# The forgetting queries and keys as four pairs of seven quarter-block products behind the last mLSTM head

## The chip, the cores and the metric

The kernel runs on one core of a Trainium2 chip. The metric is the time of one execution on the device in microseconds (us), the median of several runs. The core has engines with instruction streams of their own: TensorE (PE, matmuls; PEld, its weight loads), VectorE (DVE), ScalarE (ACT), GpSimd (POOL), and SyncE (SP), which issues nearly all DMA transfers here. On chip there are SBUF, where operands live, and PSUM, eight banks of 128 x 512 float32 that matmuls write.

## The reference

One decoder layer on 1024 tokens of width 1024. The normed input is projected by `w_in`; four mLSTM heads and eight heads of forgetting attention share it. Then come an output projection, cross-attention to 256 memory tokens, an MLP with squared ReLU, and norms. The part that matters:

```python
h = rmsnorm(x, ln1[l])
z = h @ w_in[l]
ml_qk, ml_v, ml_o, ml_i, ml_f, fx_q, fx_k, fx_v, fx_f = jnp.split(z, splits, axis=-1)
...
fq = fx_q.reshape(B, S, FX_HEADS, FX_DH)
fk = fx_k.reshape(B, S, FX_HEADS, FX_DH)
fv = fx_v.reshape(B, S, FX_HEADS, FX_DH)
fx_out = forgetting_attention(fq, fk, fv, flf).reshape(B, S, FX_W)
```

`fx_q` and `fx_k` are 512 columns each: with the features in the partitions, four blocks of 128 x 1024 tokens for the queries and four for the keys. One such block holds two heads of 64.

## The kernel before

**Numbers in two parts.** A float32 operand is cut into a rounded part `hi` and the rest `lo` (`split`: ScalarE rounds, VectorE subtracts), and a product is three matmuls, lo x hi, hi x lo and hi x hi (`mm3`, lines 186 to 188). One matmul multiplies a 128 x 128 block of weights with up to 512 columns (tokens). `h` is the input times the gain `ln1`, cut, in two halves of 512 tokens; the norm's factor is put on afterwards, from `row` (tokens in the free dimension) or `rcol` (tokens in the partitions).

**Order.** The program is one straight list of Python calls. A planner puts each engine's instructions in an order, with the program's order as their rank, and an instruction that isn't ready lets later ones pass. Tiles come from groups with a name and a number of buffers: `act` 7 (128 x 8 x 512), `w4` 5 (128 x 1024), `z4` 2, weights `wr` 2 (raw), `wh` and `wl` 3 (cut), and tiles of 128 x 512 with the numbers of

```python
BUFS = dict(a=1, b=2, c=2, d=2, e=2, f=2, p=2, y=1)
PBUFS = dict(sc=3, mm=1, m2=1, tp=2, ov=1)
```

where the second line is the eight PSUM banks. In traces the tiles of the first line are `r_a`, `r_b` and so on, and `m2` is `m`.

**The heads' stage.** `ml_project(hd)` (line 656) projects one mLSTM head: keys with convolution (`conv_silu`), forgetting queries (`fx_project(0, hd)`, line 637), the state carried from the first half of the tokens (`carried`), queries with convolution, forgetting keys (`fx_project(1, hd)`), `carry`, and the output gate. `ml_head(hd)` (line 568) is the head itself: for each of its two halves of tokens it loads a row of maxima into a tile `a` (line 575), and for four to eight key blocks it makes scores in `sc` (584), exponentials (586), a mask on GpSimd (588), the weighted scores (589), cuts them, sums them on GpSimd (593) and multiplies by the values (595); at the end the sums over partitions (606, 607) and a factor. Then it yields; the rest, its closing, is drawn by `next(closing)`: the factors become a row through DRAM (`to_row`, 623, and the load at 625) in tiles `a`, and the output goes to `mix`. The loop calls the head, then `ml_project` of the next, in which the closing's three steps stand between the projections. The eight `fx_project` calls are spread over the four heads. Each multiplies one weight block with both halves of `h` (2 x 8 x 3 matmuls of 512 columns), scales by `row`, cuts, and stores both parts to `fqk` in DRAM.

**Behind the heads.** `fx_load` fetches queries, keys and decays of a forgetting head into a `stack` (an `act` tile, after memsets at 696 and 697). `slot` (line 1026) is one step of the forgetting attention; the first 13 (`LEAD_`) make scores only. `token_major(a["w_fv"], ...)` (488, called at 1092) makes the forgetting values, 2 x 8 blocks of 24 matmuls of 256 columns; `fv_sink` evicts them in turn into `b`, `p`, `c` (137, 138) and stores them (652). Head 3's closing is drawn in two of the slots and amid the values. The slots with values (782, 801) follow.

**Seven products elsewhere.** The cross-attention's queries and the first MLP product already use quarter blocks: `left_query` and `left_up` cut the weights, `right_side` prepares the right sides, and `Pair.run` adds the seven products up.

Of the kernel before, what the change touches and what calls it, by code (L numbers as in the profile page):

```python
# [9 lines left out]
F32 = mybir.dt.float32  # L10
F32R = mybir.dt.float32r
AF = mybir.ActivationFunctionType
ALU = mybir.AluOpType
# [4 lines left out]
P = 128  # L18
T = 1024
TH = 512  # L20
D = 1024
KT = D // P
# [3 lines left out]
FXD = 64  # L26
# [18 lines left out]
def hybrid_layer(ctx: ExitStack, tc: tile.TileContext, a: dict, out: bass.AP):  # L45
    nc = tc.nc
    v, s, g = nc.vector, nc.scalar, nc.gpsimd
# [39 lines left out]
    def ps_tile(tag):  # L87
        return psum.tile([P, 512], F32, tag=tag, name=name(tag), bufs=PBUFS[tag])
# [22 lines left out]
    load = nc.sync.dma_start  # L111
# [19 lines left out]
    def split(hi, lo, src, scale=None):  # L131

        if scale is None:
            s.activation(hi, src, AF.Copy)  # L134
            return v.tensor_tensor(out=lo, in0=src, in1=hi.bitcast(F32), op=ALU.subtract)  # L135
        else:
            s.activation(hi, src, AF.Copy, scale=scale)
            return v.scalar_tensor_tensor(out=lo, in0=src, scalar=scale, in1=hi.bitcast(F32), op0=ALU.mult, op1=ALU.subtract)  # L138

    spare = {}  # L140
    last_of = {}
# [42 lines left out]
    def mm3(ps, w, x, first, last, more=False):  # L184

        nc.tensor.matmul(ps, w[1], x[0], start=first, stop=False, skip_group_check=more)  # L186
        nc.tensor.matmul(ps, w[0], x[1], start=False, stop=False, skip_group_check=more)  # L187
        nc.tensor.matmul(ps, w[0], x[0], start=False, stop=last, skip_group_check=more)  # L188

    def both(pair, f):  # L190
        return f(pair[0]), f(pair[1])
# [233 lines left out]
    def row_first():  # L425
        to_row(row, rcol, 8, rowd[0:1])
# [25 lines left out]
    def gate_rows():  # L452
        ips = []
        for hf in range(2):
            ps = mm()
            for j in range(4):
                nc.tensor.transpose(ps[:GW, j * P : (j + 1) * P], lf[:, 4 * hf + j], ident)
            s.activation(steps[:, hf * TH : hf * TH + TH], ps[:GW], AF.Copy)
        for hf in range(2):
            ips.append(mm())  # L460
            for j in range(4):
                nc.tensor.transpose(ips[hf][:MLH, j * P : (j + 1) * P], z[:, 4 * hf + j, 0:MLH], ident)
        v.tensor_tensor_scan(out=cum, data0=on, data1=steps, initial=0.0, op0=ALU.mult, op1=ALU.add)
        for hf in range(2):
            c = slice(hf * TH, hf * TH + TH)
            v.tensor_tensor(out=rel[0:MLH, c], in0=ips[hf][:MLH], in1=cum[0:MLH, c], op=ALU.subtract)
        v.tensor_tensor_scan(out=run[0:MLH], data0=rel[0:MLH], data1=rel[0:MLH], initial=0.0, op0=ALU.max, op1=ALU.max)
        top = steps
        v.tensor_tensor(out=top[0:MLH], in0=cum[0:MLH], in1=run[0:MLH], op=ALU.add)
        neg = on  # L470
        v.tensor_scalar(out=neg[0:MLH], in0=run[0:MLH], scalar1=-1.0, scalar2=None, op0=ALU.mult)
        load(rows, neg[0:MLH])
        load(rels, rel[0:MLH, :TH])
# [11 lines left out]
                load(decay[sign, p_], cut[p_].bitcast(F32))  # L485


    def token_major(w_src, sink, cs=(0, 1), between={}):

        for c in cs:  # L490
            ws = [both(weights(w_src[c, i]), lambda t: t.rearrange("p (k c) -> p k c", k=4)) for i in range(2)]
            for t in range(8):
                if t in between:
                    between[t]()
                hf, tt = divmod(t, 4)
                ps = mm()[:, 0:256]
                for k in range(KT):
                    x = both(h[hf], lambda z: z[:, k, tt * P : (tt + 1) * P])
                    mm3(ps, x, both(ws[k // 4], lambda z: z[:, k % 4]), k == 0, k == KT - 1)
                sink(t, c, ps)  # L500

    def conv_silu(n, hi, lo):
        w = weights(a["w_in"][n])
# [130 lines left out]

    fqk = dram.tile([2, 2, 4, P, T], F32, name="fqk")

    def fx_project(which, n):
        w = weights(a["w_in"][12 + 4 * which + n])
        for _, hf, ps in proj(w, h, 1):
            lo = w2("p")  # L640
            v.scalar_tensor_tensor(out=lo, in0=ps, scalar=1.0 if which else FXD ** -0.5, in1=row[:, hf * TH : hf * TH + TH], op0=ALU.mult, op1=ALU.mult)
            hi = w2("p", dt=F32R)
            split(hi, lo.bitcast(F32R), lo)
            load(fqk[which, 0, n, :, hf * TH : hf * TH + TH], hi.bitcast(F32))
            load(fqk[which, 1, n, :, hf * TH : hf * TH + TH], lo)

    fvd = dram.tile([FXH, P, 8, 2 * FXD], F32, name="fvd")

    def fv_sink(t, c, ps):
# [28 lines left out]
    token_major(a["w_mv"], mv_sink, (1,), {2: row_first, 4: gate_rows})  # L678
    gate_cols()
    banks[:] = ["mm", "tp", "m2", "tp"]  # L680
    with tc.issue_after(last_sum.ins):
# [2 lines left out]
    for hd in range(MLH):  # L684
        closing = ml_head(hd, *ready)
        next(closing)
        if hd < MLH - 1:
            ready = ml_project(hd + 1)
    row_m = row[:, :NM]
    to_row(row_m, rcol_m, 2, rowd[1:2, :NM])  # L690

# [79 lines left out]
    class Values:  # L771
# [562 lines left out]
    def bank():  # L1334
        turn[0] += 1
        return ps_tile(cycle[turn[0] % 8])

    def sub(out_, x, y, by=v):
        by.tensor_tensor(out=out_, in0=x, in1=y, op=ALU.subtract)


    def h_tile():
        t = act()
# [504 lines left out]
```

## Time and profile before

| | |
|---|---|
| runs | 1513.53, 1509.99, 1509.91 us; median 1509.99 |
| profiled execution | span 1509.2 us, 22358 instructions |
| PE busy | 1493.0 us (99%), 7806 matmuls |
| PEld busy | 1263.7 us (84%) |
| DVE busy | 1122.7 us (74%) |
| ACT busy | 757.7 us (50%) |
| POOL busy | 528.7 us (35%) |
| DMA | 303.04 MB, mean 201 GB/s |
| mean granted TensorE clock | 0.997 |

The span runs from the first to the last instruction of the one profiled execution; its own time isn't given beside it. A row of the timeline is: start in us, duration in us, engine, line, operation, tile written <- tiles read, shape, count, and in brackets the idle time before it and what ended it. A row of a group has the durations in ns as minimum/median/maximum. A row of stretches is: from:to, its length, then busy time and count of PE, PEld, DVE, ACT and POOL, the granted clock, the DMA share and GB/s. Matmuls overlap, so one's duration (some 0.39 us for 512 columns) is longer than the distance to the next.

### The profile page before, as it was taken

The numbers are of one execution on the slowest core, as the hardware profiler recorded it, in microseconds if no ns is written. First come the engines' busy times: TensorE is split into PE (matmuls) and PEld (weight loads), VectorE is DVE, ScalarE is ACT, GpSimd is POOL, SyncE is SP. The second block draws the span as 40 slices with busy tenths as digits, with TensorE's granted clock in tenths as the row PEclk, the third lists the DMA queues.
The fourth block names the chain that finished last, engine by engine and source line by source line (L and its number), as shares of the span: only waits on it lengthen the run. The fifth ranks groups of instructions, "written<-read, shape, count | busy, mean of one in ns | idle before, by whom it ended". The sixth has DMA issues, their size and how long they took to land.

```text
span 1509.2 us, 22358 instructions
## 1 busy us (share of the span) xinstructions
PE 1493.0 (99%) x7806; PEld 1263.7 (84%) x7806; DVE 1122.7 (74%) x1803; ACT 757.7 (50%) x1440; POOL 528.7 (35%) x545
## 2 busy tenths in 40 slices
PE   9999999999999999999999999999999999999997
PEld 9988888889899888788988878888888888888887
DVE  7766676664788875667767899989996678787765
ACT  7324343334688764566654467566664521122134
POOL 1003030414365441623300044454544365553312
PEclk9999999999999999999999999999999999999999
DMA  6322333435777877853354447676678677776623
GB/s 243 115 79 95 98 108 126 132 129 153 247 261 256 284 248 246 271 169 126 128 182 159 147 155 279 235 261 248 217 273 292 264 279 279 279 272 251 247 88 112
DMA packets 124276, 303.04 MB, mean 201 GB/s; under 512 B 13810, under 2 KB 28460, under 8 KB 117252
## 3 DMA queue, kind: packets, MB, share of 16 engines
q1 hardware_dynamic: 124164, 301.62, 57.3%
q8 instruction: 61, 1.00, 0.3%
q14 instruction: 51, 0.42, 0.1%
HBM read 202.75 MB, written 98.82 MB: 200 GB/s over the span
## 4 chain that ended last, share of the span: by engine, by line
PE 90%; DMA 4%; DVE 3%; ACT 1%; issue 1%; POOL 1%; POOLq 0%; DVEq 0%; SPq 0%; ACTq 0%
PE tp L186 8%; PE tp L187 8%; PE tp L188 8%; PE sc L186 6%; PE sc L188 6%; PE sc L187 6%; PE mm L186 5%; PE m L188 5%; PE m L186 5%; PE m L187 5%; PE mm L188 5%; PE mm L187 5%; PE ov L801 2%; PE ov L186 2%; PE ov L187 2%; PE ov L188 2%
## 5 line engine op out<-in xcount | busy, mean ns | idle before, releaser
L186 PE MATMUL tp<-act,wl 128*128 128x512 f32 (+1 forms) x440 | 172.6, 392 | 0.0
L187 PE MATMUL tp<-act,wh 128*128 128x512 f32 (+1 forms) x440 | 172.1, 391 | 0.0
L188 PE MATMUL tp<-act,wh 128*128 128x512 f32 (+1 forms) x440 | 171.8, 392 | 0.0
L135 DVE TENSOR_TENSOR wl<-wr,wh 128x1024 fp32r<-128x1024 f32 (+2 forms) x99 | 131.4, 1327 | 27.0 <-ACT wh L134 26.7
L134 ACT ACTIVATE wh<-wr 128x1024 fp32r<-128x1024 f32 (+2 forms) x99 | 99.8, 1008 | 85.7 <-PE tp L188 32.7
L186 PE MATMUL mm<-act,wl 128*128 128x512 f32 (+1 forms) x332 | 124.8, 376 | 2.6 <-DVE r_c L138 2.1
L188 PE MATMUL mm<-act,wh 128*128 128x512 f32 (+1 forms) x332 | 124.1, 374 | 0.0
L187 PE MATMUL mm<-act,wh 128*128 128x512 f32 (+1 forms) x332 | 123.8, 373 | 0.0
L186 PE MATMUL m<-act,wl 128*128 128x512 f32 (+1 forms) x308 | 113.8, 369 | 0.6 <-DVE wl L135 0.6
L188 PE MATMUL m<-act,wh 128*128 128x512 f32 (+1 forms) x308 | 113.8, 369 | 0.0
L187 PE MATMUL m<-act,wh 128*128 128x512 f32 (+1 forms) x308 | 113.7, 369 | 0.0
L188 PE MATMUL sc<-act,wh 128*128 128x512 f32 (+1 forms) x280 | 105.6, 377 | 0.0
L187 PE MATMUL sc<-act,wh 128*128 128x512 f32 (+1 forms) x280 | 105.6, 377 | 0.0
L186 PE MATMUL sc<-act,wl 128*128 128x512 f32 (+1 forms) x280 | 105.6, 377 | 0.0
L1612 POOL TENSOR_TENSOR z<-wr 128x256 f32<-128x256 f32 x56 | 52.9, 966 | 131.8 <-DMA wr<-w_ff2q 126.7
L188 PEld LDWEIGHTS tp<-act,wh 128*128 128x128 f32 x440 | 82.7, 188 | 19.0
L186 PEld LDWEIGHTS tp<-act,wl 128*128 128x128 f32 x440 | 82.7, 188 | 18.5
L187 PEld LDWEIGHTS tp<-act,wh 128*128 128x128 f32 x440 | 82.7, 188 | 18.2
L134 ACT ACTIVATE wh<-z 128x1024 fp32r<-128x1024 f32 (+1 forms) x54 | 55.5, 1027 | 81.8 <-POOL z L1612 62.3
L135 DVE TENSOR_TENSOR wl<-z,wh 128x1024 fp32r<-128x1024 f32 (+1 forms) x54 | 77.7, 1439 | 11.4 <-ACT wh L134 11.4
L134 ACT ACTIVATE w<-wr 128x768 fp32r<-128x768 f32 (+3 forms) x35 | 28.0, 801 | 107.4 <-PE tp L186 33.0
L186 PEld LDWEIGHTS mm<-act,wl 128*128 128x128 f32 x332 | 62.7, 189 | 14.2 <-DVE r_c L138 2.6
(734 smaller groups left out, 4387.2 us busy)
## 6 DMA issues: line engine op xcount, KB each, us to landing
act<-right SPq DMA_DIRECT2D x49, 1024.0 KB
right<-w SPq DMA_DIRECT2D x56, 256.0 KB
wr<-w_ff2q SPq DMA_DIRECT2D x28, 512.0 KB
right<-r_d SPq DMA_DIRECT2D x49, 256.0 KB
right<-r_e SPq DMA_DIRECT2D x49, 256.0 KB
act<-fqk SPq DMA_DIRECT2D x48, 256.0 KB
wr<-w_in SPq DMA_DIRECT2D x20, 512.0 KB
wr<-w_ff SPq DMA_DIRECT2D x20, 512.0 KB
```

The source lines that it names most:

```text
L134: s.activation(hi, src, AF.Copy)
L135: return v.tensor_tensor(out=lo, in0=src, in1=hi.bitcast(F32), op=ALU.subtract)
L186: nc.tensor.matmul(ps, w[1], x[0], start=first, stop=False, skip_group_check=more)
L187: nc.tensor.matmul(ps, w[0], x[1], start=False, stop=False, skip_group_check=more)
L188: nc.tensor.matmul(ps, w[0], x[0], start=False, stop=last, skip_group_check=more)
L801: nc.tensor.matmul(self.ov[:, c0:], self.fv[:, self.j], t[:, c0:], start=self.j == 0 and t is self.p[1], stop=self.last and t is self.p[0])
L1612: g.tensor_tensor(out=o, in0=x, in1=y, op=op)
```

## The change

The forgetting queries and keys leave `ml_project`. Behind the fourth head's main part stand now, in this order: the right sides from x (`first_rights`, `last_rights`: loads of x again, times the gain, differences, cut into three `act` and four `w4` tiles), the first half of the forgetting values (`fv_tiles[0]`), and 28 products (`in_jobs`). A pair is a query block and a key block, which together with both token halves make a 2 x 2 block product; seven products of quarter blocks (4 x 3 matmuls of 512 columns each) take the place of eight. `left_in` cuts the weights' quarters and their sums, `InPair.run` adds products up, and `done` cuts and stores to `fqk` as before. The steps of head 3's closing are drawn at three of the products. The second half of the values stays behind the 13 first slots. `token_major` becomes a generator of one channel block (`token_units`), the mLSTM values use it with the same steps between, and heads 0 and 2 now have their queries and keys in an `act` tile and heads 1 and 3 in four `w4`, where it was the other way round. `sub` only moves up.

```diff
-    def token_major(w_src, sink, cs=(0, 1), between={}):
...
+    def token_units(w_src, sink, c):
+
+        ws = [both(weights(w_src[c, i]), lambda t: t.rearrange("p (k c) -> p k c", k=4)) for i in range(2)]
+        for t in range(8):
...
+            sink(t, c, ps)
+            yield
...
-    def fx_project(which, n):
-        w = weights(a["w_in"][12 + 4 * which + n])
-        for _, hf, ps in proj(w, h, 1):
...
     def ml_project(hd):
-        qk = quarters(F32R) if hd % 2 else [w4(dt=F32R) for _ in range(4)]
+        qk = quarters(F32R) if hd % 2 == 0 else [w4(dt=F32R) for _ in range(4)]
...
-        fx_project(0, hd)
...
-        fx_project(1, hd)
...
+    for c in ("t1", "t2", "t3"):
+        t = act()
+        I_RIGHT[c] = [(t[:, k], t[:, 4 + k]) for k in range(4)]
+    I_RIGHT["t4"] = [(t[:, :TH], t[:, TH:]) for t in (w4(dt=F32R) for _ in range(4))]
+
+    def in_part(c, k, tag):
+
+        hf, n = int(c[1]) - 1, 4 * int(c[0]) - 4 + k
+        x = w2(tag)
+        load(x, a["x"][:, n, hf * TH : hf * TH + TH])
+        s.activation(x, x, AF.Copy, scale=vec[:, VEC["ln1"] + n :][:, 0:1])
+        return x
+
+    def first_rights(k):
+
+        x, y, z = (in_part(c, k, t) for c, t in (("11", "p"), ("12", "p"), ("22", "c")))
+        sub(x, y, x)
+        split(*I_RIGHT["t1"][k], x)
+        sub(x, z, x, g)
+        split(*I_RIGHT["t2"][k], x)
+
+    def last_rights(k):
+
+        y, z = (in_part(c, k, t) for c, t in (("12", "p"), ("22", "c")))
+        sub(y, z, y, g)
+        split(*I_RIGHT["t3"][k], y)
+        x = in_part("21", k, "p")
+        for t in I_RIGHT["t2"][k]:
+            sub(x, x, t.bitcast(F32), g)
+        split(*I_RIGHT["t4"][k], x)
+
+    fv_tiles = [token_units(a["w_fv"], fv_sink, c) for c in range(2)]
+
+    I_NAMES = {1: "11", 2: "21", 5: "t1", 6: "t2", 3: "22", 7: "t3", 4: "t4"}
+    i_cycle = ("sc", "mm", "tp", "sc", "m2", "tp", "sc", "ov")
...
+    for p_ in range(IP):
+        in_jobs += [(p_, 1)] + ([(p_ - 1, 4)] if p_ else []) + [(p_, i) for i in (5, 2, 6, 3, 7)]
+    in_jobs.append((IP - 1, 4))
...
+        def run(self, i, l):
+            r = I_RIGHT[I_NAMES[i]]
...
+            for k in range(4):
+                mm3(ps, both(l, lambda t: t[:, k]), r[k], i in (1, 5, 6) and k == 0, k == 3, True)
+            u = self.u
+            if i == 1:
+                self.p1 = w2("p")
+                s.activation(self.p1, ps, AF.Copy)
+            elif i == 2:
+                v.tensor_tensor(out=self.room("11", "a", "y"), in0=ps, in1=self.row_of("11"), op=ALU.mult)
+                self.done("11")
+            elif i == 5:
+                self.add(self.room("22", "e"), ps, self.p1)
+            elif i in (6, 3):
+                if "12" not in u:
+                    self.add(self.room("12", "f"), ps, self.p1)
...
+    CLOSINGS = ((0, 2), (0, 7), (1, 2))
+    LEAD_IN = 5
+    for k in range(4):
+        first_rights(k)
+    for k in range(4):
+        last_rights(k)
+    for _ in fv_tiles[0]:
+        pass
+    for at, (p_, i) in enumerate(in_jobs):
+        while in_prep and in_first[in_prep[0]] <= at + LEAD_IN:
+            left_in(*in_prep.pop(0))
...
+        if (p_, i) in CLOSINGS:
+            next(closing, None)
...
     for i in range(LEAD_):
         slot(False, 0)
-        if i in (1, 11):
-            next(closing, None)
-    token_major(a["w_fv"], fv_sink, between={4: lambda: next(closing, None)})
+    for _ in fv_tiles[1]:
+        pass
```

More of the change, by code (lines that the diff above doesn't have):

```diff
@@ L485, in gate_cols @@
                 load(decay[sign, p_], cut[p_].bitcast(F32))
-    def token_major(w_src, sink, cs=(0, 1), between={}):
[L490 to L500, printed above, removed]
+    def token_units(w_src, sink, c):
+        ws = [both(weights(w_src[c, i]), lambda t: t.rearrange("p (k c) -> p k c", k=4)) for i in range(2)]
+        for t in range(8):
+            hf, tt = divmod(t, 4)
+            ps = mm()[:, 0:256]
+            for k in range(KT):
+                x = both(h[hf], lambda z: z[:, k, tt * P : (tt + 1) * P])
+                mm3(ps, x, both(ws[k // 4], lambda z: z[:, k % 4]), k == 0, k == KT - 1)
+            sink(t, c, ps)
+            yield
     def conv_silu(n, hi, lo):
@@ L688, in hybrid_layer @@
             ready = ml_project(hd + 1)
+    I_RIGHT = {}
+    for c, hf, k0 in (("11", 0, 0), ("21", 0, 4), ("22", 1, 4)):
+        I_RIGHT[c] = [both(h[hf], lambda t: t[:, k0 + k]) for k in range(4)]
+    for c in ("t1", "t2", "t3"):
[8 more added lines that the diff above has]
+        return x
@@ new lines, in hybrid_layer, with left_in @@
+    in_first = {}
+    for at, (p_, i) in enumerate(in_jobs):
+        if i in I_GROUP:
+            in_first.setdefault((p_, I_GROUP[i]), at)
+    in_prep = sorted(in_first, key=in_first.get)
+    in_raws, in_cuts = {}, {}
+    def left_in(p_, group):
+        if group == 0:
+            in_raws[p_] = [sb("wr", [P, 1024], 2) for _ in range(2)]
+            for raw, n in zip(in_raws[p_], (16 + p_, 12 + p_)):
+                load(raw, a["w_in"][n])
+        r2, r1 = in_raws[p_]
+        x11, x12, x21, x22 = r1[:, :TH], r1[:, TH:], r2[:, :TH], r2[:, TH:]
+        if group == 0:
+            t = z4()[:, :T].bitcast(F32R)
+            h22, l22 = t[:, :TH], t[:, TH:]
+            split(h22, l22, x22)
+            in_cuts[p_, 4] = both((h22, l22), lambda t: t.rearrange("p (k c) -> p k c", k=4))
+        hi, lo = (sb(t, [P, 1024], 3, F32R) for t in ("wh", "wl"))
+        split(hi, lo, (r1, r2, r1)[group])
+        if group == 0:
+            by = g if p_ > 1 else v
+            by.tensor_tensor(out=x21, in0=x21, in1=x22, op=ALU.add)
+            sub(x22, x21, x11, by)
+            sub(x12, x12, x22, by)
+            sub(x11, h22.bitcast(F32), x22, by)
+            by.tensor_tensor(out=x11, in0=x11, in1=l22.bitcast(F32), op=ALU.add)
+        for e in range(2):
+            in_cuts[p_, ((1, 2), (5, 6), (7, 3))[group][e]] = both((hi, lo), lambda t: t[:, e * TH : e * TH + TH].rearrange("p (k c) -> p k c", k=4))
@@ new lines, in hybrid_layer, with __init__, room, row_of @@
+    class InPair:
+        def __init__(self, i):
+            self.i = i
+            self.u = {}
+        def room(self, c, *tags):
+            self.u[c] = rotate(*tags)
+            return self.u[c]
+        def row_of(self, c):
+            hf = int(c[1]) - 1
+            return row[:, hf * TH : hf * TH + TH]
+        def add(self, out_, ps, x):
+            v.tensor_tensor(out=out_, in0=ps, in1=x, op=ALU.add)
+        def run(self, i, l):
+            r = I_RIGHT[I_NAMES[i]]
+            at_ = {1: "a", 2: "a", 5: "c", 3: "c", 6: "b", 7: "b", 4: "b"}[i]
+            if i in (1, 5, 6):
+                setattr(self, at_, i_bank())
+            ps = getattr(self, at_)
+            for k in range(4):
[12 more added lines that the diff above has]
+                    self.add(self.room("12", "f"), ps, self.p1)
+                else:
+                    self.add(u["12"], ps, u["12"])
+                    self.scale("12")
+            elif i == 7:
+                self.add(u["22"], ps, u["22"])
+                self.scale("22")
+            elif i == 4:
+                u["21"] = self.p1
+                self.add(u["21"], ps, u["21"])
+                self.scale("21")
+        def scale(self, c):
+            g.tensor_tensor(out=self.u[c], in0=self.u[c], in1=self.row_of(c), op=ALU.mult)
+            self.done(c)
+        def done(self, c):
+            n, hf = int(c[0]) - 1, int(c[1]) - 1
+            x, at_ = self.u[c], slice(hf * TH, hf * TH + TH)
+            hi, lo = w2("d", dt=F32R), x.bitcast(F32R)
+            split(hi, lo, x, None if n else FXD ** -0.5)
+            load(fqk[n, 0, self.i, :, at_], hi.bitcast(F32))
+            load(fqk[n, 1, self.i, :, at_], x)
@@ new lines, in hybrid_layer @@
+    in_open = {}
+    CLOSINGS = ((0, 2), (0, 7), (1, 2))
[6 more added lines that the diff above has]
+        pass
+    for at, (p_, i) in enumerate(in_jobs):
+        while in_prep and in_first[in_prep[0]] <= at + LEAD_IN:
+            left_in(*in_prep.pop(0))
+        pair = in_open.setdefault(p_, None) or InPair(p_)
+        in_open[p_] = pair
+        pair.run(i, in_cuts.pop((p_, i)))
+        if i == 4:
+            del in_open[p_]
+        if (p_, i) in CLOSINGS:
+            next(closing, None)
@@ L1336, in bank @@
         return ps_tile(cycle[turn[0] % 8])
-    def sub(out_, x, y, by=v):
-        by.tensor_tensor(out=out_, in0=x, in1=y, op=ALU.subtract)
     def h_tile():
```

20 lines of the change are left out of this document (13 added, 7 removed).

## The prediction

> **What bounds the kernel now.** I read the page first, then busy time by stretches, then TensorE, the DMA queue and ScalarE in order of time between 60 and 400 us.
>
> ```profile
> PE 1493.0 (99%) x7806; PEld 1263.7 (84%) x7806; DVE 1122.7 (74%) x1803; ACT 757.7 (50%) x1440; POOL 528.7 (35%) x545
> PE 90%; DMA 4%; DVE 3%; ACT 1%; issue 1%; POOL 1%; POOLq 0%; DVEq 0%; SPq 0%; ACTq 0%
> ```
>
> TensorE is busy for 1493.0 of 1509.2 us and makes up 90% of the chain that ended last. Work taken from it is time won, as long as it never starves. So two questions decide: how much work goes, and whether the stretches that lose their filler still have something to do.
>
> The next rows are busy time by stretches: one head's cycle, and a stretch of the first MLP product, where quarter blocks and seven products are already in use.
>
> ```profile
> 184.00:253.00 69.00, 69.00 (x336) 57.43 (x335) 47.63 (x75) 26.73 (x44) 14.12 (x18) 1.00 0.32 108
> 950.00:1050.00 100.00, 100.00 (x431) 80.45 (x430) 90.24 (x97) 64.13 (x102) 48.82 (x31) 1.00 0.72 247
> ```
>
> A 512-column matmul costs 100/431 = 0.232 us. In the MLP stretch TensorE is full though VectorE is busy for 90 of 100 us.
>
> **The products: -11.1 us.** Eight blocks of 2 halves x 8 row blocks x 3 parts are 384 matmuls; four pairs x 7 products x 4 x 3 are 336. 48 x 0.232 = 11.1 us go. Cutting the weights and adding the products up, on VectorE, ScalarE and GpSimd, I cost at nothing: the MLP stretch hides the same operations at the same pace. Without that cover, VectorE's excess over 19.5 us a pair (84 x 0.232) would show four times. The 20 added loads of x are 256 KB each and leave the DMA share low; the stores into `fqk` are 32 before and after.
>
> **The heads lose two blocks each: 2 x 48 x 0.232 = 22.3 us per head.** TensorE's work in a cycle drops from 69.0 to 46.7 us. Can a head go that fast? The rows follow head 1 to head 2, DMA issues and TensorE in order of time.
>
> ```profile
> 182.59 0.32 SPq L575 DMA_DIRECT2D r_a<-rows  x1
> 190.69 0.40 PE L186 MATMUL sc<-act 128*128 128x512 f32 x1
> 230.87 0.95 PE L217 MATMUL sc<-ones,r_c 128*128 128x1 f32 x8
> 240.62 0.27 PE L249 MATMUL sc<-ident,c_fac 128*8 128x128 f32 x1
> 243.44 0.32 SPq L253 DMA_DIRECT2D r_a<-facd  x1
> 247.32 0.32 SPq L625 DMA_DIRECT2D r_a<-facd  x1
> 251.48 0.32 SPq L575 DMA_DIRECT2D r_a<-rows  x1
> ```
>
> The row of maxima (`nmb`) and the closing's two rows of factors (`fb`) share the one buffer `a`. So head 2's exponentials wait for head 1's closing. That chain is: load and use 3.3 us (estimate, a little over the 3.04 us below), scores to last sums 190.69 to 231.7 = 41.0, closing to the next row 19.8. Together 64.1 us, without the wait for TensorE's turn. Head 3, with little else on VectorE, gives the lower bound:
>
> ```profile
> 121.25 0.39 PE L186 MATMUL sc<-w,w 128*128 128x512 f32 x1
> 329.52 0.40 PE L186 MATMUL sc<-act 128*128 128x512 f32 x1
> 361.73 0.95 PE L217 MATMUL sc<-ones,r_c 128*128 128x1 f32 x8
> L696 POOL MEMSET act<- x4: 1799/1804/1806, 290.2 to 351.9; 32x2048 f32 x4
> ```
>
> It takes 33.0 us, of which two memsets of 1.8 us on GpSimd (the last at 351.9) held some 3.5; these move behind the products. 29.5 + 19.8 + 3.3 = 52.6 us. Between 52.6 and 64.1 I take 59, nearer the upper row, since the convolutions of the next head stay beside it. The chain, at 59 us hidden in 69 today, then ends last: TensorE has 46.7 us of work in it. Head 0 starts two blocks sooner, at 121.25 - 22.3 = 98.9; head 3 at 98.9 + 3 x 59 = 276 instead of 329.5.
>
> **The right sides wait for buffers.** This is the step that weighs most. Buffers of one name are handed out in the order in which the program first uses them, whoever is ready. ScalarE's evictions of the values beside head 3 show it, and TensorE at the first forgetting scores:
>
> ```profile
> 339.67 0.47 ACT L137 ACTIVATE r_p<-tp,rcol 128x256 fp32r<-128x256 f32 x1
> 341.19 0.47 ACT L137 ACTIVATE r_b<-mm,rcol 128x256 fp32r<-128x256 f32 x1 [1.05 <-PE sc L217]
> 348.50 0.47 ACT L137 ACTIVATE r_b<-tp,rcol 128x256 fp32r<-128x256 f32 x1
> 353.48 0.47 ACT L137 ACTIVATE r_p<-mm,rcol 128x256 fp32r<-128x256 f32 x1 [1.20 <-PE mm L188]
> 359.47 0.63 ACT L600 ACTIVATE r_c<-r_f 128x512 f32<-128x512 f32 x1 [3.49 <-DVE r_f L599]
> 360.01 0.46 ACT L137 ACTIVATE r_c<-m,rcol 128x256 fp32r<-128x256 f32 x1
> ```
>
> ```profile
> 354.46 0.28 PE L734 MATMUL sc<-act 128*128 128x256 f32 x1
> 370.87 0.27 PE L249 MATMUL sc<-ident,c_fac 128*8 128x128 f32 x1
> 370.89 0.42 PE L734 MATMUL sc<-act 128*128 128x384 f32 x1
> ```
>
> The value block that goes to `c` comes out only when head 3 has taken its last `c`, at L600, though the blocks after it were long out. The third score part, ready since about 355, starts 0.02 us after the closing's transposes took the `sc` bank ahead of it.
>
> In the change `first_rights(k)` takes two buffers `p` and one `c`, `last_rights(k)` two `p` and one `c`; there are two of each. The order is: head 3, eight such rounds, the first half of the values (which evict into `b`, `p`, `c` in turn), the products (whose P1 is a `p`). So the first `c` of a right side comes at head 3's L600: 359.47 - 329.52 = 30.0 us after its start, 26.5 without the memsets. Value blocks 1, 4, 7 (`p`) and 2, 5 (`c`) can't be evicted before the last round. TensorE can fill its four banks with six blocks, and then has nothing: the seventh block, the first product (bank `mm`, behind the values) and all later ones stand behind them. On SP the loads of x wait in line for their buffers, and behind them only weights that aren't needed before the products.
>
> One round, from these rows (issue, use, and medians of the operations):
>
> ```profile
> 641.70 0.32 SPq L1176 DMA_DIRECT2D r_f<-x1d  x1
> 654.03 1.45 SPq L1176 DMA_DIRECT2D r_f<-x1d  x2
> 644.74 0.72 ACT L1177 ACTIVATE r_f<-r_f,vec 128x512 f32<-128x512 f32 x1 [1.28 <-DMA r_f<-x1d]
> L134 ACT ACTIVATE r_p<-r_p x16: 612/632/634, 80.9 to 331.0; 128x512 fp32r<-128x512 f32 x16
> L135 DVE TENSOR_TENSOR r_p<-r_p,r_p x16: 679/692/1230, 82.0 to 331.7; 128x512 fp32r<-128x512 f32 x16
> L1339 POOL TENSOR_TENSOR wr<-wr,wr x22: 1280/1297/1682, 683.1 to 1147.9; 128x512 f32<-128x512 f32 x22
> L1339 DVE TENSOR_TENSOR w<-w,w x6: 679/685/693, 824.8 to 877.3; 128x512 f32<-128x512 f32 x6
> ```
>
> A first round can't load its second `p` before the round ahead gives back its first: load to use 3.04, scaling 0.72, subtraction 0.69, split 0.63 + 0.69, GpSimd's subtraction 1.30, split 0.63 + 0.69 = 8.4, with hand-overs 8.7 us. The opening round has its `p` already and needs 6.4. Four: 6.4 + 3 x 8.7 = 32.5. In a last round the longer of two chains is 3.04 + 0.72 + 2 x 1.30 + 0.63 + 0.69, with hand-overs 7.9; the eighth opens 3 x 7.9 = 23.7 later, and a value block gets its `p` and is out 2.2 after that: 58.4 us from L600. Bounds: loads of 1.94 us (the store quoted further down, the shortest transfer seen) and no hand-overs give 47; rounds of 12.3 us, as between the two issues quoted (641.70 to 654.03, with other work between), give 80. I take 58, since little else runs there. The first product can use its banks at 276 + 26.5 + 58.4 = 361.
>
> **From there on.** Left are 28 products (336 x 0.232 = 78.0), the second half of the values and the scores that were already made at the same point before (some 5 us, estimate from twelve parts of two matmuls each), less one product slipped in ahead (2.8). A value matmul costs 0.94/8 = 0.118 us by these rows:
>
> ```profile
> 391.75 0.28 PE L186 MATMUL tp<-wh,act 128*128 128x256 f32 x1
> 392.69 0.28 PE L188 MATMUL tp<-wh,act 128*128 128x256 f32 x1
> 392.80 0.49 PE L782 MATMUL tp<-ident,w 128*128 128x128 f32 x3
> ```
>
> So half of them is 8 x 24 x 0.118 = 22.6 us. The last closing moves too. Its row `fb` now stands behind the first pair's `u["11"]` (buffer `a`), its numerators hold both `f`, which the sixth and third products need, and its two transfers last:
>
> ```profile
> 371.60 1.94 DMA facd<-r_a
> 373.56 5.12 DMA r_a<-facd
> ```
>
> I add 3.7 us of waiting before the pair's seventh product, what its chain (some 18 us) exceeds the products that can go ahead of it; bounds 0 and 10. Sum: 361 + 78.0 - 2.8 + 22.6 + 5 + 3.7 = 467.5, where the values now end at 392.8: +74.7 us. The forgetting attention behind it starts as now, with two memsets of a stack (GpSimd) and its loads under the last products and values; 0, between -4 and +4.
>
> **The clock.** A stretch with a short wait, and the one after it:
>
> ```profile
> 630.00:642.50 12.50, 10.36 (x45) 8.07 (x44) 8.55 (x14) 7.63 (x15) 7.31 (x8) 1.00 0.77 263
> 642.50:645.90 3.40, 3.40 (x10) 2.63 (x10) 2.55 (x4) 2.08 (x4) 0.00 (x0) 0.50 0.89 293
> ```
>
> After some 2 us of idling the granted clock was 0.50 for 3.4 us. Restarting behind the long gap costs 3.4 x 0.5 = 1.7 us once; restarts inside the gap are free. The Trainium skill ("TensorE: Matmul & The Clock Gate", Part 1: The HAM clock gate) says that an idle window of about 3.4 us halves the clock until TensorE has been busy for as long; by that rule every gap of that length among the heads would pay too, an estimated 5 us more in all.
>
> The profiled execution's span is 1509.2 us, the median of the runs 0.8 above it. 1509.2 + 74.7 + 1.7 + 0.8 = **1586 us**, slower by 5%. Cross-check: 76 more with 11 less work means some 87 us of idle TensorE, about 36 of it among the heads (3 x 12.3) and the rest behind head 3.
>
> **Rivals.** *A, all is hidden*: right sides and heads keep ahead, and only the products count: 1510 - 11.1 + 2 for small waits = 1501. It needs buffers that go to whoever is ready, against the two readings above, or heads at 46.7 us. For it: TensorE is full now. *B, the heads keep up, the right sides don't*: 3 x 12.3 less than forecast, 1549. For it: in the stretch of the first rows VectorE is only 69% busy, so the chain may shorten with it. *C, the heads starve, the right sides are ready in time*: head 3 at 276, 33 for it with the values beside it, 78 + 22.6 + 5 of work: 415 against 392.8, 1532. *D, as forecast with rounds of 12 us*: +22, 1608.
>
> **How the numbers follow.** Forecast 0.52, A 0.12, B 0.13, C 0.08, D 0.10, and 0.05 that the terms cancel near the old time. The forecast's own range is 1562 to 1608 (heads at 54 to 64 us, rounds shorter or longer by 1 us). With B, C and D 8 in 10 lie between 1530 and 1615. A difference under 0.3% can't be told from none; faster 0.13, same 0.03, slower 0.84.
>
> **What would show it.** Right: the slices of the profile between 100 and 360 us fall from 9 to about 7 and below on TensorE; head starts 55 to 62 us apart; a gap of over 30 us behind head 3 whose releaser is a value block's eviction, with x loads 8 to 9 us apart in it; half clock after it; products then at 0.232 us. Wrong: x loads issued while heads 1 and 2 still run, value blocks evicted into `p` before the last right side, or head starts 47 us apart.

## The result: 8% slower, and the profile after

The changed kernel takes 1633.1 us (1631.9 to 1637.7), the kernel before 1510.9 us: a ratio of 1.081, with a 95% interval of 1.079 to 1.083. The forecast was 1586 us with a range from 1530 to 1615, so the sign and the place were right and the size was not: 122 us were lost instead of 76.

From the page of the changed kernel: the span, TensorE's busy time, its 40 slices and granted clock (41 us each, in tenths), and the shares of the chain that ended last.

```profile
span 1631.0 us, 22486 instructions
PE 1508.6 (93%) x7758; PEld 1268.4 (78%) x7758; DVE 1168.2 (72%) x1849; ACT 792.5 (49%) x1492; POOL 583.0 (36%) x583
...
PE   9989878706899999999999999999999999999997
...
PEclk9999889857999999999999999999999999999999
...
PE 77%; DVE 8%; DMA 8%; ACT 3%; issue 3%; POOL 1%; SPq 0%; DVEq 0%; POOLq 0%; ACTq 0%
```

The loss lies in slices 3 to 11, which were full before. TensorE idles for 1631.0 - 1508.6 = 122.4 us instead of 16.2: 106 us of the 121.8 that the span grew. The other 15.6 us are busy time, although 48 matmuls, 11.1 us, are gone: what is left runs 26.7 us longer. In DMA and VectorE's shares of the chain (8% each, 4% and 3% before) one sees who holds TensorE now.

The same as busy time by stretches (columns: window, its length, busy time and instructions of TensorE, its weight loads, VectorE, ScalarE and GpSimd, then granted clock, DMA share, GB/s). Of the changed kernel: the heads, from there to the first product, and from there to the end of the values.

```profile
75.00:329.00 254.00, 213.18 (x1058) 177.87 (x1058) 159.21 (x252) 90.35 (x155) 52.63 (x71) 0.92 0.20 63
329.00:389.00 60.00, 8.81 (x50) 8.31 (x50) 18.74 (x32) 26.25 (x41) 19.24 (x15) 0.54 0.33 98
389.00:510.00 121.00, 111.03 (x558) 91.78 (x559) 71.46 (x110) 40.47 (x77) 55.60 (x43) 0.97 0.62 207
```

Of the kernel before: the heads, and from there to the end of the values.

```profile
75.00:362.50 287.50, 287.50 (x1479) 243.12 (x1477) 185.71 (x291) 108.23 (x182) 64.58 (x79) 1.00 0.34 111
362.50:393.00 30.50, 29.09 (x231) 28.14 (x231) 19.43 (x55) 13.89 (x37) 8.74 (x12) 1.00 0.74 233
```

The heads take 254 us for 1058 matmuls, at 84% busy; the emptiest stretch is the 60 us behind them, with no engine busy for half of it. The values end 117 us later than before (510 against 393); the last 4.8 us are lost behind them, mostly in the MLP stage.

**The wait behind head 3.** First TensorE's longest wait between 320 and 400 us, then pieces of the chain that ended last (start, length, what).

```profile
PE m L189 <- DVE r_c L138: 43.4, 1, 43.4
```

```profile
327.16 0.64 ACT r_c L601
...
328.97 2.81 DMA r_c<-x
...
334.13 2.69 DMA r_p<-x
...
343.22 2.67 DMA r_p<-x
...
352.22 2.59 DMA r_p<-x
...
362.86 3.36 DMA r_p<-x
...
370.16 2.87 DMA r_p<-x
...
378.20 3.00 DMA r_p<-x
...
387.63 1.24 DVE wl L135
```

The first product, in TensorE's order of time:

```profile
388.91 0.50 PE L189 MATMUL sc<-act,wl 128*128 128x512 f32 x1 [1.94 <-DVE wl L135]
```

This is the forecast's third step as it was written. The first x for a `c` is loaded at 328.97, once head 3 has taken its last `c` (327.16). The first rounds are 9.1 and 9.0 us apart (334.13, 343.22, 352.22; forecast 8.7), the last ones 7.3 and 8.0 (362.86, 370.16, 378.20; forecast 7.9), and 10.6 us lie between the two kinds. TensorE's wait of 43.4 us is ended by a value block's eviction into `c`. The first product starts at 388.91, 61.7 us behind the last `c`; the forecast was 58.4.

**The heads.** The first exponentials of each head in the changed kernel (ScalarE in order of time).

```profile
109.30 0.70 ACT L587 ACTIVATE r_b<-r_a,gcol 128x512 f32<-128x512 f32 x1
176.32 0.72 ACT L587 ACTIVATE r_b<-r_a,gcol 128x512 f32<-128x512 f32 x1 [1.65 <-DMA r_a<-rows]
236.89 0.72 ACT L587 ACTIVATE r_b<-r_a,gcol 128x512 f32<-128x512 f32 x1 [1.96 <-DMA r_a<-rows]
302.56 0.72 ACT L587 ACTIVATE r_b<-r_a,gcol 128x512 f32<-128x512 f32 x1 [0.69 <-DMA r_a<-rows]
```

They come 67.0, 60.6 and 65.7 us apart, 64.4 in the mean (66.0 by the heads' first scores), where 59 was taken between 52.6 and 64.1. From head 1 on it is the row of maxima (`r_a<-rows`) that ScalarE waits for last.

### The profile page after: what moved, and what is told of

Read it like the earlier page. It is cut to its first block, busy times and chain, and to the rows that moved or that the text cites. A ratio compares the mean times of both kernels' runs of the same rounds, so it can differ in the third digit from the quotient of the medians.

```text
span 1631.0 us, 22486 instructions
## 1 busy us (share of the span) xinstructions
PE 1508.6 (93%) x7758; PEld 1268.4 (78%) x7758; DVE 1168.2 (72%) x1849; ACT 792.5 (49%) x1492; POOL 583.0 (36%) x583
## 4 chain that ended last, share of the span: by engine, by line
PE 77%; DVE 8%; DMA 8%; ACT 3%; issue 3%; POOL 1%; SPq 0%; DVEq 0%; POOLq 0%; ACTq 0%
PE sc L189 6%; PE sc L190 6%; PE sc L191 6%; PE tp L189 6%; PE tp L190 6%; PE tp L191 6%; PE mm L189 5%; PE mm L191 5%; PE mm L190 5%; PE m L190 4%; PE m L189 4%; PE m L191 4%; PE ov L958 2%; PE ov L190 2%; PE ov L191 2%
## 5 line engine op out<-in xcount | busy, mean ns | idle before, releaser
L135 DVE TENSOR_TENSOR wl<-wr,wh 128x1024 fp32r<-128x1024 f32 (+2 forms) x103 | 137.5, 1336 | 39.7 <-ACT wh L134 39.5
L134 ACT ACTIVATE wh<-wr 128x1024 fp32r<-128x1024 f32 (+2 forms) x103 | 104.1, 1012 | 117.4 <-PE tp L191 47.6
L189 PE MATMUL tp<-act,wl 128*128 128x512 f32 (+1 forms) x372 | 147.9, 398 | 3.1 <-DVE w L661 3.1
L190 PE MATMUL tp<-act,wh 128*128 128x512 f32 (+1 forms) x372 | 147.5, 396 | 0.0
L191 PE MATMUL tp<-act,wh 128*128 128x512 f32 (+1 forms) x372 | 147.0, 397 | 0.0
L189 PE MATMUL sc<-act,wl 128*128 128x512 f32 (+1 forms) x332 | 127.0, 383 | 9.4 <-DVE wl L135 6.4
L190 PE MATMUL sc<-act,wh 128*128 128x512 f32 (+1 forms) x332 | 125.8, 379 | 0.0
L191 PE MATMUL sc<-act,wh 128*128 128x512 f32 (+1 forms) x332 | 125.6, 378 | 0.0
L191 PE MATMUL m<-act,wh 128*128 128x512 f32 (+1 forms) x288 | 106.2, 369 | 0.0
L189 PE MATMUL m<-act,wl 128*128 128x512 f32 (+1 forms) x288 | 106.2, 369 | 0.0
L190 PE MATMUL m<-act,wh 128*128 128x512 f32 (+1 forms) x288 | 106.1, 368 | 0.0
L189 PEld LDWEIGHTS tp<-act,wl 128*128 128x128 f32 x372 | 71.0, 191 | 20.3 <-DVE w L661 3.5
L135 DVE TENSOR_TENSOR wl<-z,wh 128x1024 fp32r<-128x1024 f32 (+1 forms) x54 | 76.6, 1419 | 11.7 <-ACT wh L134 11.7
L191 PEld LDWEIGHTS tp<-act,wh 128*128 128x128 f32 x372 | 70.8, 190 | 16.8
L190 PEld LDWEIGHTS tp<-act,wh 128*128 128x128 f32 x372 | 70.9, 191 | 16.3
```

## The experiments

Each stands beside a run of the kernel before, which took 1510.9 to 1512.9 us. The edits are made to the changed kernel (1633.1 us), or where it says "the same" to the one ahead. Each is a single run, and the changed kernel's own four runs lie 5.7 us apart, so differences of that size say little by themselves.

**The third x tile in the convolutions' buffers.**

```
-        x, y, z = (in_part(c, k, t) for c, t in (("11", "p"), ("12", "p"), ("22", "c")))
+        x, y, z = (in_part(c, k, t) for c, t in (("11", "p"), ("12", "p"), ("22", "z")))
```

The same in `last_rights`; "z" stands for half a tile `z4`.

> The third x tile of each round of right sides (the one that was a buffer c) now comes from the convolutions' buffers, which are free from about 281 us; nothing else changes. Theory (the rounds wait for head 3's last c, 327 us in the trace): the four first rounds run beside head 3, only four last rounds of 7.3 to 8 us stand behind it, the first product comes at about 360 instead of 388.9, and the time falls by some 28 us, to 1605 (1598 to 1612). Rival (the tiles that the right sides go to come free only with head 3's end, or the loads of x are what limits): first product within 5 us of 388.9, time above 1626.

1611.9 us, 21 less, at the edge of the theory's range and far from the rival's. The first product comes at 352.13, 37 us sooner. Then TensorE waits again (its waits between 320 and 400 us):

```profile
PE tp L189 <- DVE r_p L138: 11.7, 1, 11.7
PE sc L189 <- DVE wl L135: 4.6, 1, 4.6
```

A value block's eviction into `p`, still behind the last rounds, holds the bank of the second product. And head 3 took its last `c` at 336.98 instead of 327.16, with the first rounds beside it on ScalarE and VectorE. So it was the order of `c` that held the rounds, and part of what that gave went into the next buffer in line.

**The closings' factors in `p`.**

```
-            fb = w2("a")
+            fb = w2("p")
```

> The closings' two rows of factors take the buffer p, which the forgetting projections have given up, instead of the one buffer a that also holds the row of maxima; nothing else changes. Theory (the heads' pace is the chain through a): the heads' first exponentials come some 50 us apart (46.7 us of TensorE's work and a few small waits) instead of 64.4; head 3 ends about 40 us sooner, the wait behind it stays at about 62 us, and the time falls to about 1593 (1583 to 1605). Rival (the heads go at the pace of the convolutions' chain on VectorE and ScalarE): 60 us apart or more, time above 1620.

1620.5 us, 13 less: the time lies just on the rival's side, the distances fit neither. Its heads' first exponentials:

```profile
110.29 0.70 ACT L587 ACTIVATE r_b<-r_a,gcol 128x512 f32<-128x512 f32 x1
157.69 0.70 ACT L587 ACTIVATE r_b<-r_a,gcol 128x512 f32<-128x512 f32 x1
234.25 0.71 ACT L587 ACTIVATE r_b<-r_a,gcol 128x512 f32<-128x512 f32 x1
282.37 0.71 ACT L587 ACTIVATE r_b<-r_a,gcol 128x512 f32<-128x512 f32 x1
```

No load stands ahead of them any more, and two of the three distances are 47.4 and 48.1 us, TensorE's own 46.7 and little else. The third is 76.6 us, and head 3 ends only 6 us sooner (its last `c` at 321.59). Something else holds head 2. VectorE's evictions of the projections into the convolutions' buffers, in the same run, show a part of it, and GpSimd's row shows what the query convolution waits for:

```profile
155.39 0.69 DVE L508 TENSOR_TENSOR z<-m,row 128x512 f32<-128x512 f32 x1
188.28 0.68 DVE L508 TENSOR_TENSOR z<-tp,row 128x512 f32<-128x512 f32 x1
202.97 0.68 DVE L508 TENSOR_TENSOR z<-m,row 128x512 f32<-128x512 f32 x1
220.38 0.68 DVE L508 TENSOR_TENSOR z<-tp,row 128x512 f32<-128x512 f32 x1
```

```profile
201.19 0.10 POOL L506 MEMSET z<- 128x3 f32 x1 [1.82 <-DVE z L516]
```

Head 2's key convolution has its first half at 155 and its second at 188. Its query convolution gets a buffer `z4` only at 201, when L516 of the key convolution is done with it, because each of the two uses both; its evictions come at 203 and 220, and the exponentials follow at 234. The 33 us between the key convolution's halves are not explained by these buffers: TensorE was busy with other work for most of that time (29.33 of the 32.90 us from 155.40 to 188.30). And the edit has a price of its own: TensorE's longest wait in these heads, 6.4 us in two pieces, is for the state, cut into a `p` (L135), in which the factors now are too.

**Both.**

> Both edits: factors in p, third x tile in the convolutions' buffers. Theory: the two gains add, 28 + 40 us, 1565 (1553 to 1580). Rival (factors and right sides now meet at p, and the closing or the rounds wait for each other): less than the larger of the two alone.

1602.1 us, 31 less: the two gains, 21 and 13, nearly add, but neither was as large as expected.

**Whole blocks behind head 3.** `first_rights`, `last_rights` and the products are replaced by the eight `fx_project` blocks of before, placed in the program behind the first half of the values, with the closings at three of them.

> The eight projections leave the heads as in the change, but stay whole blocks behind head 3 and the first half of the values: no products, no right sides. Theory: the heads starve as in the changed kernel (last sums of head 3 within 6 us of 328.6) except that head 3 finds blocks to fill it; behind it no gap. Left at 328.6 are ten value blocks, 384 matmuls and the scores, 28.3 + 89.3 + 5 = 122.6 us, less what slips into head 3: second values end at 435 to 451 where the kernel before has 392.8, time 1552 to 1573. That would put 60 to 80 us of the loss on the right sides and products, and 45 to 60 on the empty heads. Rival (the empty heads are the whole loss): 1620 or more; rival (the right sides are the whole loss): 1520 or less.

1563.1 us (span 1561.2), as expected. The values end 52 us later than before. From 329 us on:

```profile
329.00:445.00 116.00, 116.00 (x613) 98.52 (x614) 49.81 (x98) 32.46 (x65) 8.74 (x12) 1.00 0.62 206
```

TensorE is full. So the whole loss of 52.0 us (1561.2 - 1509.2) lies in the emptied heads.

**The products without their right sides.**

```
+    for c, (hf, k0) in zip(("t1", "t2", "t3", "t4"), ((1, 0), (0, 0), (1, 4), (0, 4))):
+        I_RIGHT[c] = [both(h[hf], lambda t: t[:, k0 + k]) for k in range(4)]
...
-    for k in range(4):
-        first_rights(k)
-    for k in range(4):
-        last_rights(k)
```

> The right sides t1 to t4 are left out: the products take slices of the normalised input in their place, so the forgetting queries and keys are not the reference's; every product, addition, store and place stays. Theory (the loss behind head 3 is the wait for the right sides, and the products themselves cost what their matmuls cost): no gap behind head 3; against the plain blocks behind (1563) 11.1 us less TensorE work and up to 11 us of waits among the products, 1552 to 1566. Rival (cutting the weights, adding up and the last closing hold the products as much as the right sides do): above 1580.

1569.3 us (span 1567.5), 3 us above the theory's range. The same stretch as above:

```profile
329.00:445.00 116.00, 109.83 (x570) 92.48 (x570) 74.80 (x119) 40.26 (x76) 43.99 (x34) 0.97 0.62 208
```

There is no gap, but the 11.1 us of work that the products save do not come out: 6.2 us of idling in this stretch and its clock of 0.97 take most of them, and the values end no sooner (0.4 us) than with whole blocks. From the values' end to its own end it takes 6.3 us more than the kernel before (1122.7 against 1116.4); all kernels here that have the products lose 3 to 7 us behind that point, the kernel with whole blocks loses none. With the changed kernel's 1631.0 this splits the loss: 52.0 us for the emptied heads, 6.3 for products in place of blocks (11.1 won, 17.4 lost), 63.5 for the right sides.

**All values in the heads**, two blocks at each of the eight places where an `fx_project` stood, and

```
-        o = rotate("b", "p", "c").bitcast(F32R)
+        o = w2("p").bitcast(F32R)
```

> All sixteen value blocks are traced inside the heads, two at each of the eight places where the forgetting projections stood, and go out through p alone; the right sides and products stay as in the change. Theory (the heads starve for lack of filler): ten of the sixteen blocks, 10 x 24 x 0.118 = 28.3 us, leave the stretch behind head 3 and use TensorE's idle time in the heads, whose 512-column matmuls also run less at half clock; the gap behind head 3 stays at about 60 us: 1608 (1596 to 1618). Rival (the heads are as much longer as they are fuller, since evictions into p or VectorE limit them): 1626 or more.

1618.2 us, 15 less, just past the theory's range. The heads do take the values, but head 3 begins 17 us later for it (319.99 against 302.56).

**The same with quicker right sides.** The third x in `z4`, all `t3` ahead of all `t4` and subtracted on VectorE instead of GpSimd, the last x in `c`, and its two subtractions on GpSimd and VectorE in turn:

```
-            sub(x, x, t.bitcast(F32), g)
+            sub(x, x, t.bitcast(F32), by)
```

> As values_in_heads, and the right sides loosened: third x tile in the convolutions' buffers; all four t3 ahead of all four t4, x of t4 in c, the subtractions shared out to VectorE. Theory (the rounds are serial through two buffers p and one c, and GpSimd's subtractions): first rights beside head 3, last ones some 5 us each instead of 8, the first two products run in the gap: 1608 - 28 - 12 = 1568 (1552 to 1582). Rival (the tiles t3 and t4 go to are held until head 3's end, and the loads then cost as much again): above 1590.

1585.9 us, 32 less than the one above, 4 short of the theory's range. So the right sides' rounds could still be shortened. Which of the four edits gave how much was not taken apart.

**The same with the factors in `p`.**

> As values_quick, and the closings' factors in p instead of a. Theory (the chain through a is what is left of the heads' waits once TensorE has filler): 10 to 20 us less than values_quick. Rival (p now carries the state, the values, the factors and the right sides, and becomes the single buffer that a was): no less, or more.

1605.6 us, 20 more than without: the rival. In `p` now meet the state, the values, the factors, the right sides and the products' P1; the heads come 73.8, 70.3 and 77.4 us apart, and head 3 takes its last `c` 19.9 us later (365.42 against 345.48). Which of the users of `p` holds the others was not taken apart.

**The values ahead of the right sides**, the two loops exchanged.

> The first half of the values is traced ahead of the right sides instead of behind them. Theory (the right sides themselves are late, since their rounds begin at head 3's last c): the values are out some 40 us sooner, but the first product still comes 60 us behind head 3's last c or a little later, 1630 to 1642. Rival (what holds TensorE is mainly that the values' evictions stand behind the rounds in the line for p and c): the values and the first two products fill the gap, 1605 to 1618.

1628.8 us, 4 less, a little under the theory's range and far from the rival's. TensorE's waits in that run between 320 and 400 us:

```profile
PE mm L189 <- ACT r_p L794: 18.2, 1, 18.2
PE tp L189 <- ACT act L134: 16.4, 4, 5.1
PE sc L189 <- ACT act L134: 5.4, 4, 1.6
```

With the values out of the way the first product, which needs no right side, starts at 325 and not 60 us behind head 3 as the theory had it. The next ones wait row block by row block for the right sides (`act`) themselves, and the longest wait is for the eviction of a first product into `p` (L794). That the values were stuck was a symptom.

**The convolutions with one tap of four.**

```
-        for j in range(1, 4):
+        for j in range(3, 3):
```

> The last three of the four taps of the convolution are left out (three VectorE operations of 1.25 us in each of the eight convolutions), so the heads' queries and keys are not the reference's. Theory (the heads' pace is the chain through the buffer a): heads 1 to 3 still come 61 to 65 us apart, time within 6 us of 1633. Rival (the pace is the two convolutions, one after the other through the same two buffers): 3.8 us off each, 7.6 us a head, head 3 ends 20 to 30 us sooner, 1603 to 1613.

1610.7 us, 22 less: in the time, the rival. Head 0 begins 9.5 us sooner (99.81) and the heads come 65.0, 58.5 and 57.7 us apart, 4 us less each in the mean, where the rival named 7.6. And ScalarE still waits last for the row of maxima at the starts of heads 1 to 3, so the chain through `a` ends last here too. At head 2:

```profile
223.35 0.72 ACT L587 ACTIVATE r_b<-r_a,gcol 128x512 f32<-128x512 f32 x1 [2.18 <-DMA r_a<-rows]
```

The edit also takes some 30 us of work from VectorE (24 operations of 1.25 us), which may shorten that chain too. This run does not part the two.

**One tap, and the factors in `p`.**

> Both: three taps left out, and the closings' factors in p instead of a. With factors in p alone head 3 ended only 6 us sooner. Theory (two chains of nearly the same length, through a and through the convolutions' buffers; each alone holds the heads): both together give more than the sum of the two alone, head 3 ends 25 to 40 us sooner, 1593 to 1608. Rival (a third thing, TensorE's own order or p, holds the heads): no more than 5 us better than the better one alone.

1588.5 us, 45 less, where the two alone gave 22 and 13. Its first exponentials:

```profile
99.34 0.71 ACT L587 ACTIVATE r_b<-r_a,gcol 128x512 f32<-128x512 f32 x1
145.33 0.71 ACT L587 ACTIVATE r_b<-r_a,gcol 128x512 f32<-128x512 f32 x1
204.79 0.71 ACT L587 ACTIVATE r_b<-r_a,gcol 128x512 f32<-128x512 f32 x1
256.14 0.71 ACT L587 ACTIVATE r_b<-r_a,gcol 128x512 f32<-128x512 f32 x1
```

They come 46.0, 59.5 and 51.4 us apart. That the two together give more than their sum fits two chains of almost one length, where loosening one shows the other: the one through `a`, and one through VectorE and the convolutions. Whether it is the two buffers `z4` or VectorE's load that makes the second is not shown.

**The counter of banks.**

```
+    turn[0] += 4
     row_m = row[:, :NM]
```

> One number: the counter of banks is set four on behind the products. The products take 28 banks where the blocks took 32, so the MLP stage, whose banks go round in eight by the same counter, starts half a round away from where it did before; four on puts it back. Theory (the 4.8 us that the changed kernel loses between the end of the values and its own end, in the MLP stage alone, come from that half round): the stage runs as before, 1633 - 5 = 1628. Rival (they come from the other counters that the products move, or from what memory the stage finds): 1632 to 1634.

1636.0 us: the theory falls. The time is still lost, 6.7 us instead of 4.8 from the values' end to the kernel's. What it comes from stays open; TensorE's waits there are for what VectorE cuts and adds, and in the changed kernel VectorE's busy time in the MLP stage is that of before (373 and 372 us).

None of these beats the kernel before; the nearest keeps whole blocks and is 52 us behind it.

## Why the forecast was wrong, step by step

Profile against profile, the forecast was +76.4 us and 121.8 were measured. The miss of 45.4 us is mostly in two terms: the heads' pace and start (24.6 us), and the products' cutting and adding at nothing (14.4 us for their whole stretch). The wait for the right sides, which the forecast called the step that weighs most, was right to 3.3 us.

**The products, -11.1 us, with the cutting and adding at nothing.** The work did go, but the cover was gone with it: the MLP stage, from which the price of nothing was read, has a full TensorE ahead of each product, and here nothing was queued. TensorE's longest waits between 389 and 510 us in the changed kernel are for the cuts of the weights (L135) and the adding up (L781):

```profile
PE sc L189 <- DVE wl L135: 4.4, 2, 2.4
PE sc L189 <- DVE r_f L781: 3.0, 1, 3.0
PE sc L189 <- DVE r_e L781: 1.6, 2, 0.8
```

From 388.91 to the end of the values at 509.8 it took 120.9 us instead of 106.5, 14.4 more. By estimate 2.8 of them are the product that was to slip in ahead and did not, some 6 are idling beyond the 3.7 us taken for the closing (121.00 - 111.03 = 10.0 in all), and some 3 are two stretches at half clock, in which TensorE was busy for 3.40 and 3.04 us; the rest stays open. Without the right sides the products still lost more than they gained.

**The heads at 59 us.** Mis-sized, and its chain incomplete. These are the first scores of heads 0 and 3 in the changed kernel:

```profile
109.78 0.68 PE L189 MATMUL sc<-act 128*128 128x512 f32 x3
```

```profile
307.63 0.40 PE L189 MATMUL sc<-w,w 128*128 128x512 f32 x1
```

Head 0 was to start two blocks sooner, at 98.9; it started at 109.8. It has no head ahead of it, so nothing of the chain through `a` applies; with three taps less in the convolutions it came 9.5 us sooner. Three distances of 66.0 in the mean instead of 59 made head 3 another 20.8 us late, 31.6 in all. It was 7.0 us quicker to its last `c` than taken, which leaves 24.6. The forecast named one chain, through `a`. The runs show that this is not all: with `a` loosened head 3 ended 6 us sooner, with shorter convolutions some 22, and with both more than the sum. The bound from above, 64.1, was the better choice. The lower one was read from head 3, which has little beside it; the heads before it always have the next head's projections and convolutions there.

**The right sides' wait, 58.4 us.** Right in cause, place and size (61.7 us). Loosening `c` moved the first product 37 us; exchanging the order of the values moved the time by 4 us; leaving the right sides out took 63.5 us away. The forecast laid more weight on the values' evictions in the line than they deserve: they hold TensorE in the trace, but behind them stand the same right sides.

**The clock, 1.7 us once.** This step failed. It priced one restart, behind the long gap. The busy time of what was left grew by 26.7 us, and up to 445.5 us the trace has nine stretches of half clock, where the kernel before has none so early. Pieces of two of them, in the heads and among the products, and the sum over all nine (134.9 to 138.3, 186.1 to 196.3, 230.5 to 240.7, 261.2 to 264.6, 281.7 to 285.1, 295.3 to 305.6, 329.4 to 384.1, 425.0 to 428.4 and 442.1 to 445.5 us):

```profile
234.90:240.20 5.30, 5.28 (x12) 4.13 (x13) 2.84 (x6) 2.70 (x6) 0.88 (x3) 0.50 0.37 135
424.90:428.10 3.20, 3.16 (x8) 2.51 (x9) 1.13 (x2) 0.63 (x1) 1.28 (x1) 0.52 0.00 0
```

```profile
sum 102.40, PE 40.50 PEld 34.42 DVE 50.98 ACT 41.22 POOL 30.92; mean PE 4.50 PEld 3.82 DVE 5.66 ACT 4.58 POOL 3.44
```

Twelve matmuls in 5.28 us are 0.44 us each, where a row of them at full clock takes 0.232. So an estimated 19 of the 26.7 us are the clock: 40.50 x (1 - 0.232/0.44). The rest, matmuls that stand alone (0.40 us each) among it, stays open. These 19 us are no further term beside the others; they lie in the heads, the gap and the products. The Trainium skill's rule quoted in the prediction ("TensorE: Matmul & The Clock Gate", Part 1: The HAM clock gate) would have given an estimated 5 us more; that was the right direction and too little as well.

**The rest.** The 4.8 us behind the values were in no step. 24.6 + 3.3 + 14.4 + 4.8 make 47.1, less the 1.7 us of clock that the forecast had beside them, 45.4.

**The rivals.** C, "the heads starve, the right sides are ready", was priced at 1532 us; the kernel without right sides is that case and took 1569. It put 33 us on the heads and took 11 off for the products; measured were 52.0 for the emptied heads and 6.3 more for the products. Rival and forecast thus shared one error, the price of the starving heads with the products behind them, +22 instead of +58, and a range drawn from rivals that shared it could not hold the time.

## What to carry to other kernels

When filler leaves a stage, the stage falls to the pace of its dependency chains. Look for all chains that are nearly as long (a buffer with too few copies can make one) and take the upper bound: here loosening a single chain gave less than its share, and the measured pace lay at the upper bound or above it. A price of nothing that is read from a full stage need not hold in one that is not full. Right sides that are made out of buffers which the stage ahead still uses are late by as many rounds as they have: count their buffers in the order in which the program hands them out, before counting the matmuls that they save.

## What the hardware showed that was not expected

The granted clock fell to half without one long wait. The nine half-clock stretches listed above begin at distances of 15, 13, 9, 6, 4, 10, 28 and 5 times 3.413 us from one to the next. So the clock changes on a grid. Here are two pairs of neighbouring windows of that grid (columns as above), and the longest wait in the first window of each pair:

```profile
172.44:175.86 3.42, 1.81 (x8) 1.50 (x9) 2.31 (x5) 1.86 (x3) 0.00 (x0) 1.00 0.86 323
175.86:179.27 3.41, 3.41 (x16) 2.75 (x15) 2.29 (x5) 2.68 (x5) 0.88 (x3) 1.00 0.26 98
257.79:261.20 3.41, 1.71 (x11) 1.45 (x12) 3.41 (x7) 1.57 (x2) 1.89 (x3) 1.00 0.00 0
261.20:264.62 3.42, 3.42 (x9) 2.67 (x9) 2.59 (x5) 0.90 (x2) 0.73 (x1) 0.50 0.00 0
```

```profile
174.05 0.50 PE L189 MATMUL tp<-act,wl 128*128 128x512 f32 x1 [3.07 <-DVE w L661]
259.59 0.44 PE L190 MATMUL ov<-r_e,act 128*128 128x384 f32 x1 [1.70 <-DVE r_e L135]
```

A wait of 3.07 us, spread over two windows that were each busy for more than half, cost no clock. Waits of at most 1.70 us, in a window that was busy for half, cost it in the next window, in which TensorE did not wait at all. In this trace every window at full clock with TensorE busy for at most 50% was followed by half clock, and none with 51% or more. It is no sharp rule: in the run with one tap of four a window at 45% stayed without consequence and one at 86% was followed by half clock.

The Trainium skill ("TensorE: Matmul & The Clock Gate", A second HAM failure mode: psum-queue depth-cycling) says that short idling between groups, often enough, makes the clock swing between half and full. This trace agrees: at 261.20 the clock fell with no wait as long as the window of 3.4 us that the same page's Part 1 names.
